# A layer norm that takes its mean from the first tiles: four norms of a two-block network on one core

## The chip, the cores and the metric

The kernel runs on one core of a Trainium2 chip. The metric is the device time of one launch in microseconds, the median of several runs. The kernel before took 2532.76 us (three runs, 2528.5 to 2535.85).

Engines are named as the profile names them: PE is TensorE's matmul (PEld its weight load), DVE is VectorE, ACT is ScalarE, SP is SyncE, whose queue starts the DMA transfers. An engine works its own list of instructions in order and waits at an instruction until what it needs is there.

## The reference

Two blocks follow one another; the change touches only the second. That is a trunk of two layers over 256 tokens of width 1024 and, beside them, 256 context tokens. A layer is

```python
def _layer_norm(x, g, b):
    mu = jnp.mean(xf, axis=-1, keepdims=True)
    var = jnp.mean(jnp.square(xf - mu), axis=-1, keepdims=True)
    return ((xf - mu) * lax.rsqrt(var + NORM_EPS) * g + b)
...
    y, yc = _token_mixer(x * (1 + scale1) + shift1, xc * (1 + cscale1) + cshift1, p, cos, sin, last)
    x = _layer_norm(DN_ALPHA * x + gate1 * y, p['ln1_g'], p['ln1_b'])
    x = _layer_norm(DN_ALPHA * x + gate2 * _conv_ffn(x * (1 + scale2) + shift2, p), p['ln2_g'], p['ln2_b'])
    if last:
        return x, None
    xc = _layer_norm(DN_ALPHA * xc + cgate1 * yc, p['ln1_g'], p['ln1_b'])
    xc = _layer_norm(DN_ALPHA * xc + cgate2 * _conv_ffn(xc * (1 + cscale2) + cshift2, p), p['ln2_g'], p['ln2_b'])
```

The token mixer is a gated linear attention, a latent attention and a convolution side by side, merged by an output projection; `_conv_ffn` is an up projection to twice 2816 columns, a short convolution, a gate and a down projection. The first layer needs both streams (0 is x, 1 is the context), the second only x.

## The kernel before

Features lie on the 128 partitions and tokens along the free dimension, so a stream is 8 tiles of 128 x 256 and a norm over features is a sum over partitions and tiles. Weights come from HBM in blocks (`wraw`, four buffers). ScalarE casts each block to a high part `wh` (line 284), VectorE subtracts to get the low part `wl` (line 285), three buffers each, so a cast waits until TensorE has released the block three before. Activations are split in the same way (`hx`: line 312 on ScalarE, line 313 on VectorE), and each product is three matmuls (lines 320, 321, 322).

`project` is the output projection of a layer and `down` the down projection of its feed-forward part, each one stream at a time. After each output tile an epilogue adds the residual (line 1225) and, from the second tile on, adds the tile into a running total (lines 1315 and 1383). When all eight tiles of a stream are there, `ln` runs: one matmul of the total with a matrix of -1/D gives minus the mean on all partitions (line 1170); each tile is shifted by it (VectorE, line 1172) and squared (ScalarE, line 1174, into one of four `lt` buffers); its column sums go to PSUM by small matmuls with a vector of ones (line 374, four records of the profile a tile). Then come the variance (line 384), a reciprocal root by integer start and two refinements on VectorE (lines 361 to 367), two transposes that spread the result over the partitions (line 379), and one product a tile (line 1180). `modulate` applies scale and shift (ScalarE, line 1145) and splits the result into `hx` for the next dense stage; the last norm instead goes to line 1889 (ScalarE) and from there to the output by DMA. In layer 1's start, line 1507 onwards make the gates of the linear attention.

`beside` is called within a norm and lets the next piece of work take a step: stream 1's projection beside stream 0's norm, stream 0's up projection beside stream 1's norm. In layer 1 there is one stream, so the norm after `project` has nothing beside it, and that after `down` is the end of the program. The order of instructions on each engine comes from a scheduler that works on the whole program; it isn't written out by hand.

Of the kernel before, what the change touches and what calls it, by code (L numbers as in the profile page):

```python
# [16 lines left out]
AF = mybir.ActivationFunctionType  # L17
ALU = mybir.AluOpType
# [3 lines left out]
P = 128  # L22
D = 1024
KT = 8
S = 256
# [3 lines left out]
EPS = 1e-6  # L29
# [166 lines left out]
class Body:  # L196
# [968 lines left out]
    def ln(self, pool, s, w, eps, total, beside):  # L1165
# [13 lines left out]
        for k in range(KT):  # L1179
            nc.vector.tensor_tensor(s[k], s[k], R, ALU.mult)  # L1180
            if k % 2:
                beside()

    def begin(self, l, hx):


        nc, tc = self.nc, self.tc
        key = f"v2{l}"
        n = 2 - l
        g = SimpleNamespace(hx=hx, hq=[(h[:, : S * n], w[:, : S * n]) for h, w in hx], od={}, ud={}, hb={}, ahead=True)  # L1190
        pool = lambda es, n, **k: es.enter_context(tc.tile_pool(name=f"{n}{l}", bufs=1, **k))
        g.mix, g.mix2, g.cin = [ExitStack() for _ in range(3)]
        g.lp = lp = pool(g.mix, "mix")
        self.mp = lambda: self.t(lp, [P, 2, 512], tag="M", bufs=4)

        for v in ("b_gates", "b_conv", "b_r", "conv_dw", "gla_norm_g"):
            a, k, L = self.vat[key][v]
            g.hb[v] = self.t(lp, [P, k * L], tag="h_" + v)
            nc.vector.tensor_scalar(g.hb[v], self.vt[key][:, a : a + k * L], 0.5, None, ALU.mult)
        x = self.v(key, "b_qk")[:, :, 0]  # L1200
        g.hb["b_qk"] = self.t(lp, x.shape, tag="n_b_qk")
        nc.vector.tensor_scalar(g.hb["b_qk"], x, 128.0 ** -0.5, None, ALU.mult)
        self.bp = pool(g.mix2, "mixb")
        self.ncv = 2 if l == 0 else 3
        g.Rc = self.psum(S * n, "sx")
        V = lambda v, k, i=0: self.vc(key, v, k, i)
        cin = pool(g.cin, "cin", side="right")
        g.decay, pre = self.gla_gates(l, cin, lp, hx, g.hb, V)
        g.work = self.conv_in(l, cin, g, V, list(range(n)), pre)
        return g  # L1210

    def layer(self, l, g, mod, xd, xo, nxt, late):


        nc, tc = self.nc, self.tc
        key = f"v2{l}"
        V = lambda n, k, i=0: self.vc(key, n, k, i)
        full = [0, 1] if l == 0 else [0]
# [58 lines left out]
        def beside(gp, i):  # L1277
            if l == 0:
                self.ada_all(1)
            taps(gp)  # L1280
# [22 lines left out]
        h2 = self.modulated()  # L1303
        s = [m2[:, i, :W] for m2 in [self.mp() for _ in range(4)] for i in range(2)]
        tiles = lambda st: [t[:, sl(st)] for t in s]
        sums = {}

        def project(st):
            x = tiles(st)
            sums[st] = total = self.t(lp, [P, S], tag="lt", bufs=4)  # L1310

            def epi_o(m, ps):
                residual(x[m], st, m, ps, xd, 16)
                if m:
                    nc.vector.tensor_tensor(total, x[0] if m == 1 else total, x[m], ALU.add)

            return self.dense_steps(f"w_o{l}", range(4), mx, epi_o, tok=lambda m: sl(st))

# [30 lines left out]
        for st in full:  # L1349
# [9 lines left out]
                    work = up(range(0, 6), sl(0))  # L1359
            beside = lambda: next(work, None)  # L1360
            x = tiles(st)
            self.ln(lp, x, S, EPS / 2, sums[st], beside)
            self.modulate(lp, x, sc, sh, st, h2, beside)
            for k in range(KT):
                nc.vector.tensor_scalar(x[k], x[k], V("ln1_g", k), V("ln1_b", k), ALU.mult, ALU.add)
# [9 lines left out]

        def down(st):
            x = tiles(st)
            sums[st] = total = self.t(lf, [P, S], tag="lt", bufs=4)

            def epi_d(m, ps):  # L1380
                residual(x[m], st, m, ps, xo, 40)
                if m:
                    nc.vector.tensor_tensor(total, x[0] if m == 1 else total, x[m], ALU.add)

            return self.dense_steps(f"w_dn{l}", range(KT), gx, epi_d, tok=lambda m: sl(st))

        work, out = down(0), None
        for st in full:
# [8 lines left out]
                    work = islice(out.work, 4)  # L1397
            beside = lambda: next(work, None)
            x = tiles(st)
            self.ln(lf, x, S, EPS / 2, sums[st], beside)  # L1400
            h = nxt(lf, x, st, beside)
            out = out or h
        return out, late2
# [601 lines left out]
```

## Time and profile before

| | before |
|---|---|
| median of 3 runs | 2532.76 us (2528.5 to 2535.85) |
| profiled execution | 2538.2 us, its span 2536.3 us |
| TensorE, VectorE, ScalarE busy | 97%, 72%, 50% of the span |
| mean granted TensorE clock | 0.984 |
| chain that ended last | TensorE 86%, VectorE 7%, DMA 3%, ScalarE 2% |
| largest groups of the chain | lines 320, 321, 322: 22%, 21%, 21%; line 374: 2% |

The table says where time could be won at all: TensorE is nearly always busy, so the share of the other engines counts only in the short stretches where TensorE waits for them. Four norms are touched by the change, and the prediction calls them by letters: A, layer 0, after `project` of stream 1 (about 1395 to 1450 us); B, layer 0, after `down` of stream 1 (about 1785 to 1870); C, layer 1, after `project` (about 2314 to 2340); D, layer 1, after `down`, the last of the program (from 2516). In a row of the timeline "x8" stands for eight instructions in a run, and what is in brackets is how long the engine stood idle before the row and which engine and line released it.

### The profile page before, as it was taken

What the parts mean: (1) busy time and instruction counts of PE and PEld (TensorE: products, weight loads), DVE (VectorE), ACT (ScalarE), POOL (GpSimd) and SP (SyncE); (2) the same over time, 40 slices, a digit from 0 to 9 for tenths busy, and PEclk for the clock granted to TensorE, in tenths of its full rate; (3) what the DMA queues carried; (4) which work ended last, traced back from release to release, by engine and by line L of the source; (5) the groups of instructions that cost most, each with busy time, mean ns of one, the idle gap of its engine ahead of it and who ended that gap; (6) DMA issues with size and microseconds to landing.
All of it is one profiled execution on the core that took longest, in us unless ns stands there. A gap on an engine that the chain in (4) does not pass through costs nothing.

```text
span 2536.3 us, 45917 instructions
## 1 busy us (share of the span) xinstructions
PE 2459.2 (97%) x18416; PEld 2108.9 (83%) x18416; DVE 1817.8 (72%) x3390; ACT 1260.5 (50%) x2252; POOL 0.2 (0%) x4
## 2 busy tenths in 40 slices
PE   7999999999999999999999999999989999998998
PEld 7577878998788888666889998899878897798997
DVE  8566568856777688786636876656786688777884
ACT  5432345655456532554433654444655645555653
POOL 0000000000000000000000000000000000000000
PEclk9999999999999999999999999999999999998998
DMA  6566466554321222432334542256342332365663
GB/s 205 193 232 233 141 200 202 189 182 142 108 88 59 67 94 80 163 121 79 125 108 158 171 150 92 98 187 192 132 145 74 105 129 70 125 197 167 193 198 110
DMA packets 125782, 361.53 MB, mean 143 GB/s; under 512 B 14209, under 2 KB 39681, under 8 KB 125441
## 3 DMA queue, kind: packets, MB, share of 16 engines
q1 hardware_dynamic: 125568, 358.60, 43.2%
q8 instruction: 145, 2.38, 0.4%
q14 instruction: 69, 0.56, 0.1%
HBM read 344.08 MB, written 14.46 MB: 141 GB/s over the span
## 4 chain that ended last, share of the span: by engine, by line
PE 86%; DVE 7%; DMA 3%; ACT 2%; issue 1%; SPq 0%; ACTq 0%; DVEq 0%
PE mm L320 22%; PE mm L322 21%; PE mm L321 21%; PE aux L374 2%; PE sy L1110 2%; DVE wl L285 2%; DVE cv L1461 2%; PE aux L1780 1%; PE aux L1661 1%; PE sy L1793 1%; PE aux L1779 1%; PE aux L1617 1%; PE mm L1582 1%; PE aux L748 1%; PE mm L1580 1%
## 5 line engine op out<-in xcount | busy, mean ns | idle before, releaser
L284 ACT CAST wh<-wraw 128x1024 fp32r<-128x1024 f32 (+3 forms) x544 | 543.5, 1000 | 739.2 <-PE mm L321 626.0
L285 DVE TENSOR_TENSOR wl<-wraw,wh 128x1024 fp32r<-128x1024 f32 (+3 forms) x544 | 631.9, 1163 | 327.2 <-ACT wh L284 313.9
L320 PE MATMUL mm<-hx,wh 128*128 128x256 f32 (+1 forms) x1816 | 607.3, 335 | 9.1 <-ACT wh L284 3.4
L322 PE MATMUL mm<-hx,wl 128*128 128x256 f32 (+1 forms) x1816 | 602.9, 333 | 5.6 <-DVE wl L285 5.4
L321 PE MATMUL mm<-hx,wh 128*128 128x256 f32 (+1 forms) x1816 | 603.5, 333 | 1.5 <-DVE hx L313 1.5
L320 PEld LDWEIGHTS mm<-hx,wh 128*128 128x128 f32 x1816 | 345.5, 191 | 47.0 <-issue 4.1
L322 PEld LDWEIGHTS mm<-hx,wl 128*128 128x128 f32 x1816 | 344.8, 190 | 43.1 <-DVE wl L285 7.0
L321 PEld LDWEIGHTS mm<-hx,wh 128*128 128x128 f32 x1816 | 345.3, 190 | 37.9 <-issue 4.0
L1461 DVE SCALAR_TENSOR_TENSOR cv<-u,h_conv_dw,cv 128x512 f32<-128x512 f32 (+1 forms) x480 | 295.4, 616 | 8.6
L320 PE MATMUL mm<-b,wh 128*128 128x256 f32 x688 | 200.1, 292 | 2.1 <-ACT b L312 1.8
L322 PE MATMUL mm<-b,wl 128*128 128x256 f32 x688 | 196.3, 286 | 1.4 <-DVE wl L285 1.4
L321 PE MATMUL mm<-b,wh 128*128 128x256 f32 x688 | 195.7, 285 | 0.6 <-DVE b L313 0.6
L320 PEld LDWEIGHTS mm<-b,wh 128*128 128x128 f32 x688 | 132.0, 193 | 19.2 <-issue 11.5
L321 PE MATMUL mm<-gx,wh 128*128 128x256 f32 x528 | 147.9, 280 | 0.0
L322 PE MATMUL mm<-gx,wl 128*128 128x256 f32 x528 | 147.8, 280 | 0.0
L320 PE MATMUL mm<-gx,wh 128*128 128x256 f32 x528 | 147.7, 280 | 0.0
L321 PE MATMUL mm<-sp,wh 128*128 128x256 f32 (+1 forms) x448 | 141.0, 315 | 0.1
L322 PE MATMUL mm<-sp,wl 128*128 128x256 f32 (+1 forms) x448 | 140.7, 314 | 0.1
L320 PE MATMUL mm<-sp,wh 128*128 128x256 f32 (+1 forms) x448 | 140.6, 314 | 0.0
L322 PEld LDWEIGHTS mm<-b,wl 128*128 128x128 f32 x688 | 131.9, 192 | 7.6 <-DVE wl L285 2.6
L321 PEld LDWEIGHTS mm<-b,wh 128*128 128x128 f32 x688 | 131.7, 192 | 4.4 <-DVE b L313 2.1
L322 PEld LDWEIGHTS mm<-gx,wl 128*128 128x128 f32 x528 | 99.4, 188 | 0.0
(546 smaller groups left out, 4476.6 us busy)
## 6 DMA issues: line engine op xcount, KB each, us to landing
wraw<-w_up SPq DMA_DIRECT2D x100, 512.0 KB, 3.5
wraw<-w_ada SPq DMA_DIRECT2D x88, 512.0 KB, 4.8
wraw<-w_gates SPq DMA_DIRECT2D x48, 512.0 KB, 3.5
wraw<-w_dn SPq DMA_DIRECT2D x48, 512.0 KB, 3.6
wraw<-f_up SPq DMA_DIRECT2D x44, 512.0 KB, 3.5
wraw<-w_in SPq DMA_DIRECT2D x34, 512.0 KB, 4.0
wraw<-w_conv SPq DMA_DIRECT2D x32, 512.0 KB, 3.6
wraw<-w_o SPq DMA_DIRECT2D x24, 512.0 KB, 3.5
```

The source lines that it names most:

```text
L284: nc.scalar.copy(h, raw)
L285: nc.vector.tensor_tensor(l, raw, h.bitcast(F32), ALU.subtract)
L320: mm(ps, wh, xh, start=first, stop=False)
L321: mm(ps, wh, xl, start=False, stop=False)
L322: mm(ps, wl, xh, start=False, stop=last)
L374: self.nc.tensor.matmul(pc[:, t : t + 1], sq[:, t * P : t * P + P], self.ones[:, 0:1], start=first and t == 0, stop=last and t == n - 1)
L748: mm(ps[q, i], lhs(8 * b + i, q), rhs(8 * b + i, q), start=True, stop=True)
L1110: nc.tensor.matmul(ps[q], self.sc[:, c : c + 32], w[:, i], start=j == 0 and k < nt, stop=j == len(lot) - 1 and k >= KT - nt)
L1461: nc.vector.scalar_tensor_tensor(r(o), u[:, :, j : j + S], dw(j), r(o), ALU.mult, ALU.add)
L1580: mm(ps, xh[:, tk], wh, start=kk == 0, stop=False)
L1582: mm(ps, xh[:, tk], wl, start=False, stop=kk == KT - 1)
L1617: mm(ps[r : r + b, s, j], ka[:, a : a + b], qa[:, c : c + b], start=True, stop=True)
```

## The change

For the last stream of each layer (`st == full[-1]`: stream 1 in layer 0, stream 0 in layer 1) the norms after `project` and after `down` are done by a new function `ln_ahead`. It takes as a provisional mean that of the first n tiles (n = 6 after `project`, 7 after `down`): the total of those tiles is scaled by 8/n on ScalarE and multiplied with the matrix of -1/D. All n tiles are shifted, squared and summed as soon as tile n-1 has its residual, and each later tile as soon as it has its own. The sums of the later tiles' shifted values are taken too (`pc[:, 2:4]`); from them follows how far the provisional mean is off. The variance is the mean square less the square of that offset, and the result is x times y plus b, where y is the reciprocal root and b is minus the offset times y. So a tile gets a product and an addition where it got a product.

```diff
+    def ln_ahead(self, x, total, n, pool):
...
+        def shifted(k):
+            nc.vector.tensor_tensor(x[k], x[k], st.R, ALU.add)
+            q = self.t(pool, [P, S], tag="lt", bufs=4)
+            nc.scalar.activation(q, x[k], AF.Square)
+            if k >= n:
+                self.colsum(st.pc[:, 2:4], x[k], False, False)
+            self.colsum(st.pc[:, 0:2], q, k == 0, k == KT - 1)
+
+        def taken(m):
+            if 0 < m < n:
+                nc.vector.tensor_tensor(total, x[0] if m == 1 else total, x[m], ALU.add)
+            if m == n - 1:
+                nc.scalar.activation(total, total, AF.Copy, scale=KT / n)
+                st.R, st.pc = self.psum(S, "aux"), self.psum(4, "aux")
+                nc.tensor.matmul(st.R, self.cc("negd", "c0"), total, start=True, stop=True)
+                for k in range(n):
+                    shifted(k)
+            elif m >= n:
+                shifted(m)
+
+        def done(eps, beside):
+            v, w, b = [self.t(self.sm, [P, 2], tag=t) for t in ("rsv2", "lnw", "lnb")]
+            nc.scalar.activation(w, st.pc[:, 2:4], AF.Square, scale=1.0 / D)
+            nc.vector.tensor_scalar(v, st.pc[:, 0:2], 1.0 / D, eps, ALU.mult, ALU.add)
+            nc.vector.tensor_tensor(v, v, w, ALU.subtract)
+            y = self.rsqrt(v, 2)
+            nc.vector.scalar_tensor_tensor(b, st.pc[:, 2:4], -1.0 / D, y, ALU.mult, ALU.mult)
+            beside()
+            R = self.psum(2 * S, "aux")
+            for i, c in enumerate((y, b)):
+                for t in range(2):
+                    self.rowcast(c, t, R[:, i * S + t * P : i * S + t * P + P])
+            beside()
+            for k in range(KT):
+                nc.vector.tensor_tensor(x[k], x[k], R[:, :S], ALU.mult)
+                nc.vector.tensor_tensor(x[k], x[k], R[:, S:], ALU.add)
+                if k % 2:
+                    beside()
...
         def project(st):
             x = tiles(st)
-            sums[st] = total = self.t(lp, [P, S], tag="lt", bufs=4)
+            taken = add_up(st, x, lp, 6)
...
-                if m:
-                    nc.vector.tensor_tensor(total, x[0] if m == 1 else total, x[m], ALU.add)
+                taken(m)
...
         def down(st):
             x = tiles(st)
-            sums[st] = total = self.t(lf, [P, S], tag="lt", bufs=4)
+            taken = add_up(st, x, lf, 7)
```

`add_up` returns `taken` of `ln_ahead` for the last stream and the old total otherwise; the old norm stays for stream 0 of layer 0. ScalarE's list has 24 table loads in the whole program where it had 22; the two new ones stand in the gate logs (line 1523 before).

The order moves with it. On ScalarE at A, the list before has stream 0's modulate (line 1145, with its cast, line 312) to the end, and then stream 1's eight squares, of which two stand here (line 1174; `M` are the tiles, `fsh` and `fsc` shift and scale, `wraw` and `wh` a weight block).

```order
L1145 ACTIVATE lt_14177<-M_13543,fsh_13535,fsc_13534 128x256
L1145 ACTIVATE lt_14181<-M_13544,fsh_13535,fsc_13534 128x256
L312 CAST hx_13539<-lt_14177 128x256
L312 CAST hx_13539<-lt_14181 128x256
L284 CAST wh_14344<-wraw_14342 128x1024
L1145 ACTIVATE lt_14185<-M_13544,fsh_13535,fsc_13534 128x256
L312 CAST hx_13539<-lt_14185 128x256
L284 CAST wh_14384<-wraw_14382 128x1024
L1174 ACTIVATE lt_14250<-M_13541 128x256
L1174 ACTIVATE lt_14255<-M_13541 128x256
```
In the changed kernel (line 1203 the scaling, line 1194 a square) the same place reads:

```order
L284 CAST wh_14313<-wraw_14311 128x1024
L284 CAST wh_14354<-wraw_14352 128x1024
L1203 ACTIVATE lt_13817<-lt_13817 128x256
L1194 ACTIVATE lt_14094<-M_13541 128x256
L1194 ACTIVATE lt_14099<-M_13541 128x256
L284 CAST wh_14396<-wraw_14394 128x1024
L1194 ACTIVATE lt_14104<-M_13542 128x256
L1194 ACTIVATE lt_14109<-M_13542 128x256
L1194 ACTIVATE lt_14114<-M_13543 128x256
L1194 ACTIVATE lt_14119<-M_13543 128x256
L1145 ACTIVATE lt_14123<-M_13541,fsh_13535,fsc_13534 128x256
L1145 ACTIVATE lt_14127<-M_13541,fsh_13535,fsc_13534 128x256
```
The squares of the first six tiles now stand ahead of the first modulate of stream 0, with one weight cast among them.

On TensorE at D, the list before ends the down projection (`gx` with `wh` and `wl`), and then has the mean and the column sums, of which two of the eight rows stand here.

```order
L321 MATMUL mm_26550<-gx_24739,wh_26613 128x256
L322 MATMUL mm_26550<-gx_24738,wl_26614 128x256
L320 MATMUL mm_26550<-gx_24740,wh_26613 128x256
L321 MATMUL mm_26550<-gx_24741,wh_26613 128x256
L322 MATMUL mm_26550<-gx_24740,wl_26614 128x256
L1170 MATMUL aux_26640<-lt_25934,v_c_2_75 128x256
L374 MATMUL aux_26641<-v_c_2_75,lt_26644 128x1 x2
L374 MATMUL aux_26641<-v_c_2_75,lt_26649 128x1 x2
```
In the changed kernel the first column sums stand within the last tile's matmuls (seven such rows in all, the mean matmul, line 1205, ahead of them):

```order
L320 MATMUL mm_26642<-gx_24229,wh_26645 128x256
L374 MATMUL aux_26605<-v_c_2_75,lt_26608 128x1 x2
L321 MATMUL mm_26642<-gx_24230,wh_26645 128x256
L322 MATMUL mm_26642<-gx_24229,wl_26646 128x256
L320 MATMUL mm_26642<-gx_24231,wh_26675 128x256
L374 MATMUL aux_26605<-v_c_2_75,lt_26613 128x1 x2
```
and after its last matmul only the last tile's two sums, of the shifted tile (`ring`) and of its square (`lt`), and four transposes are left:

```order
L320 MATMUL mm_26642<-gx_24793,wh_26705 128x256
L321 MATMUL mm_26642<-gx_24794,wh_26705 128x256
L322 MATMUL mm_26642<-gx_24793,wl_26706 128x256
L374 MATMUL aux_26605<-v_c_2_75,ring_25986 128x1 x2
L374 MATMUL aux_26605<-v_c_2_75,lt_26730 128x1 x2
L379 MATMUL aux_26757<-v_c_2_75,rsy_4329_26744 128x128 x2
L379 MATMUL aux_26757<-v_c_2_75,lnb_26740 128x128 x2
```
Eight column sums and the mean came after the last matmul; now two sums do, and the transposes are four, two of the root and two of `lnb`.

## Rows read from the trace of the kernel before

**Rows 1.** The page: span, TensorE's busy time, the chain that ended last by engine.
```profile
span 2536.3 us, 45917 instructions
...
PE 2459.2 (97%) x18416; PEld 2108.9 (83%) x18416; DVE 1817.8 (72%) x3390; ACT 1260.5 (50%) x2252; POOL 0.2 (0%) x4
...
PE 86%; DVE 7%; DMA 3%; ACT 2%; issue 1%; SPq 0%; ACTq 0%; DVEq 0%
```

**Rows 2.** Timeline at D: start us, us, engine line op out<-in, idle before <-releaser.
```profile
2516.44 0.28 PE L322 MATMUL mm<-gx,wl 128*128 128x256 f32 x1
...
2516.76 0.48 DVE L1225 SCALAR_TENSOR_TENSOR ring<-mm,mod,ring 128x256 f32<-128x256 f32 x1 [5.87 <-PE mm L322]
...
2518.50 2.74 DVE L1172 TENSOR_TENSOR ring<-ring,aux 128x256 f32<-128x256 f32 x8 [0.79 <-PE aux L1170]
...
2519.42 6.50 PE L374 MATMUL aux<-v_c,lt 128*128 128x1 f32 x32 [0.96 <-ACT lt L1174]
...
2525.95 0.16 DVE L384 TENSOR_SCALAR rsv<-aux 128x2 f32<-128x2 f32 x1 [4.71 <-PE aux L374]
...
2528.23 0.66 PE L379 MATMUL aux<-v_c,rsy 128*128 128x128 f32 x2 [2.32 <-DVE rsy L367]
...
2529.00 2.74 DVE L1180 TENSOR_TENSOR ring<-ring,aux 128x256 f32<-128x256 f32 x8 [0.91 <-PE aux L379]
...
2529.46 4.04 ACT L1889 ACTIVATE ring<-ring,v_v 128x256 f32<-128x256 f32 x8 [6.45 <-DVE ring L1180]
```

**Rows 3.** Timeline at C.
```profile
2314.14 0.28 PE L322 MATMUL mm<-sp,wl 128*128 128x256 f32 x1
...
2323.50 0.16 DVE L384 TENSOR_SCALAR rsv<-aux 128x2 f32<-128x2 f32 x1 [4.21 <-PE aux L374]
...
2328.06 0.69 ACT L312 CAST hx<-lt 128x256 fp32r<-128x256 f32 x2
...
2328.50 1.01 PE L320 MATMUL mm<-hx,wh 128*128 128x256 f32 x3 [2.06 <-ACT hx L312]
```

**Rows 4.** Windows at A (two) and B: busy us (instructions) of each engine, PEclk, DMA.
```profile
1405.00:1415.00 10.00, 8.08 (x49) 7.47 (x48) 7.31 (x20) 4.26 (x10) 0.00 (x0) 0.78 0.51 175
1447.00:1449.00 2.00, 0.40 (x4) 0.19 (x2) 2.00 (x6) 1.71 (x3) 0.00 (x0) 1.00 0.62 193
1836.00:1838.00 2.00, 0.00 (x0) 0.00 (x0) 2.00 (x5) 2.00 (x4) 0.00 (x0) 0.83 0.00 0
```

**Rows 5.** Chain of waits within 1370 to 1440 (stream 0's norm among matmuls).
```profile
1379.15 0.57 PE aux L1170 x2
...
1384.57 0.34 PE aux L374 x4
```

**Rows 6.** Window at C.
```profile
2320.00:2332.00 12.00, 7.46 (x33) 6.71 (x33) 7.12 (x27) 5.35 (x14) 0.00 (x0) 0.50 0.00 1
```

**Rows 7.** Timeline at A.
```profile
1394.83 1.09 ACT L1145 ACTIVATE lt<-M,fsh,fsc 128x256 f32<-128x256 f32 x2 [0.18 <-DVE M L1180]
...
1400.33 0.48 DVE L1225 SCALAR_TENSOR_TENSOR M<-mm,mod,M 128x256 f32<-128x256 f32 x1
...
1405.80 0.28 PE L320 MATMUL mm<-hx,wh 128*128 128x256 f32 x1
...
1405.88 1.05 ACT L284 CAST wh<-wraw 128x1024 fp32r<-128x1024 f32 x1 [0.62 <-PE mm L321]
...
1409.36 5.83 PE L374 MATMUL aux<-v_c,lt 128*128 128x1 f32 x32 [1.37 <-ACT lt L1174]
```

**Rows 8.** Timeline at B.
```profile
1797.87 0.50 PE L374 MATMUL aux<-v_c,lt 128*128 128x1 f32 x4
...
1817.06 0.43 DVE L313 TENSOR_TENSOR hx<-lt,hx 128x256 fp32r<-128x256 f32 x1
...
1822.36 1.28 ACT L1523 ACT_TABLE_LOAD   x1
...
1823.66 1.06 ACT L1523 ACTIVATE sp<-sp 128x1024 f32<-128x1024 f32 x1
```

More of the change, by code (lines that the diff above doesn't have):

```diff
@@ L1182, in ln @@
                 beside()
+    def ln_ahead(self, x, total, n, pool):
+        nc = self.nc
+        st = SimpleNamespace()
+        def shifted(k):
[34 more added lines that the diff above has]
+                    beside()
+        return taken, done
     def begin(self, l, hx):
@@ L1305, in layer, with add_up, taken, norm @@
         tiles = lambda st: [t[:, sl(st)] for t in s]
-        sums = {}
+        sums, ahead = {}, []
+        def add_up(st, x, pool, n):
+            sums[st] = total = self.t(pool, [P, S], tag="lt", bufs=4)
+            if st == full[-1]:
+                taken, done = self.ln_ahead(x, total, n, pool)
+                ahead.append(done)
+                return taken
+            def taken(m):
+                if m:
+                    nc.vector.tensor_tensor(total, x[0] if m == 1 else total, x[m], ALU.add)
+            return taken
+        def norm(pool, x, st, beside):
+            if st == full[-1]:
+                ahead.pop()(EPS / 2, beside)
+            else:
+                self.ln(pool, x, S, EPS / 2, sums[st], beside)
         def project(st):
             x = tiles(st)
-            sums[st] = total = self.t(lp, [P, S], tag="lt", bufs=4)
+            taken = add_up(st, x, lp, 6)
             def epi_o(m, ps):
                 residual(x[m], st, m, ps, xd, 16)
-                if m:
-                    nc.vector.tensor_tensor(total, x[0] if m == 1 else total, x[m], ALU.add)
+                taken(m)
             return self.dense_steps(f"w_o{l}", range(4), mx, epi_o, tok=lambda m: sl(st))
@@ L1361, in layer @@
             x = tiles(st)
-            self.ln(lp, x, S, EPS / 2, sums[st], beside)
+            norm(lp, x, st, beside)
             self.modulate(lp, x, sc, sh, st, h2, beside)
@@ L1377, in down @@
             x = tiles(st)
-            sums[st] = total = self.t(lf, [P, S], tag="lt", bufs=4)
+            taken = add_up(st, x, lf, 7)
             def epi_d(m, ps):
                 residual(x[m], st, m, ps, xo, 40)
-                if m:
-                    nc.vector.tensor_tensor(total, x[0] if m == 1 else total, x[m], ALU.add)
+                taken(m)
             return self.dense_steps(f"w_dn{l}", range(KT), gx, epi_d, tok=lambda m: sl(st))
@@ L1399, in layer @@
             x = tiles(st)
-            self.ln(lf, x, S, EPS / 2, sums[st], beside)
+            norm(lf, x, st, beside)
             h = nxt(lf, x, st, beside)
```

## The prediction

> **What bounds the kernel now.** I read the page first. TensorE is busy for 2459.2 of the 2536.3 us of the span, and in the chain that ended last it holds 86% and VectorE 7% [rows 1]. So a change that takes work off other engines pays only where TensorE stands still, and every instruction that is added to TensorE costs its duration. Next I read the timelines around the four norms that are changed. I call them A (layer 0, after the output projection, stream 1), B (layer 0, after the down projection, stream 1), C (layer 1, after the output projection) and D (the last norm of the program). They differ in what lies beside them.
>
> D stands alone. The last down matmul ends at 2516.44 + 0.28 = 2516.72, and the program ends 19.6 us later [rows 1, 2]. In between the reader sees a serial chain: residual, total, mean, eight shifts, column sums for 6.50 us, 2.28 us of small VectorE operations for the reciprocal root (2525.95 to 2528.23), eight products, output. C is alone as well, but only until the first up matmul: the last projection matmul ends at 2314.42, the small operations start at 2323.50 (9.08 later), and the first matmul on hx starts at 2328.50 [rows 3]. At A and B stream 1's norm lies beside stream 0's work, so there the question is which engine's queue is full. At A, 40 us later, TensorE is busy for 0.40 of 2 us while VectorE is busy for all of it, and at B a stretch of 2 us has no matmul at all and VectorE full [rows 4]. These two places pay for VectorE work.
>
> **D, step by step.** Added to TensorE ahead of the last matmul: one mean matmul and seven tiles' column sums. Where stream 0's norm is already interleaved with matmuls, the pair of records of a mean matmul costs 0.57 in the chain and a tile's column sums 0.34 [rows 5]. So 0.57 + 7 x 0.34 = 2.95 us, and the last matmul ends that much later. The seven shifts and squares themselves lie beside the last tile's matmuls, during which VectorE is free (its residual waits 5.87 us for TensorE [rows 2]).
> After it: residual 0.52 (with its start), shift 0.42, then the square; from the first shift to the first column sum before it is 0.92 (2518.50 to 2519.42), so the last square's sum starts 0.54 + 0.92 = 1.46 after the last matmul, and with about 0.5 for itself the small operations start at about 2.1. They are 13 where 11 were: the one before the first row cast adds 2.28 / 11 = 0.2, so the cast starts at 2.1 + 2.5 = 4.6. A cast takes 0.77 until its reader starts (2528.23 to 2529.00); the second one follows. The first product starts at 5.4, the first addition perhaps 0.3 later than it could. Then 16 VectorE operations at 2.74 / 8 = 0.34 end at about 11.3, where 8 took 2.74. ScalarE's last output operation takes another 0.6, and from its end to the end of the span stay 2.8 us (2529.46 + 4.04 = 2533.50 to 2536.3). Together 14.7 after the last matmul instead of 19.6: -4.9 + 2.95 = **-1.9 us**. If nothing came early, the eight additions would cost 2.74 more on VectorE, of which some 1.2 hides because ScalarE's outputs were pacing (4.04 against 2.74 [rows 2]), plus 0.2, plus 0.3: +2.0 at worst. At best the column sums slip into gaps that the weight loads leave and D gives -2.5.
>
> **C.** Six tiles' sums stand ahead of the last matmul: 0.57 + 6 x 0.34 = 2.6 later. The last two tiles bring four sums behind it. By the same steps as at D the small operations start about 2.5 after the last matmul, so 5.2 where 9.08 was: -3.9, plus 0.2 for one more operation. The eight additions (2.74) lie on VectorE between the cast and the up matmuls; there VectorE was busy 7.12 of 12 us, at a TensorE clock of 0.50 [rows 6], so the 4.9 idle us take them. If that cover were gone they would cost 1.9, because VectorE would pace hx. Something returns later, where the next weight block waits for VectorE; I take 0.7. **-3.0**, between -3.7 (nothing returns) and -1.1 (that cover gone).
>
> **A.** Off TensorE goes the run of column sums at a lower clock (5.83 us for 32 records [rows 7]); on it come ten tiles' sums (eight of squares, two of shifted tiles) at 0.34, 3.4: -2.4. VectorE gets eight additions and loses two totals: 6 x 0.34 = +2.0, and it is the engine that TensorE waits for in this stage [rows 4], so I count 2.0 in full. The third term is order. Before, stream 0's modulate starts at 1394.83, ahead of tile 5's residual at 1400.33, and the first hx matmul comes at 1405.80 [rows 7]. Now six squares stand ahead of that modulate on ScalarE. They can't start before tile 5's residual (1400.81), total, scaling and mean matmul, about 1402.4; with six squares at 0.42 and a weight cast of 1.05 between them the modulate starts near 1406.3, and the first hx is ready near 1407.3. TensorE wants it at 1405.80 + 2.6 = 1408.4. So 10 us of slack shrink to one, while two more squares and weight casts (each about 0.4 and 1.05 [rows 7]) stand between the following modulates. A wait there is between 0 and 4; I take 2. **+1.6**, from -4.3 (no wait, VectorE's work hidden, and the 1.9 idle us of 1405 to 1415 [rows 4] close as well) to +3.6.
>
> **B.** Here VectorE is full. Eight additions less one total: 7 x 0.34 = +2.4 on the engine that TensorE waits for [rows 4]. Column sums were already interleaved, at 0.50 a tile [rows 8]; nine sets at 0.34 now stand for eight at 0.50: -0.9. ScalarE's list has two more table loads in the gate logs. Such a load takes 1.28 us on the engine, and the activation next to it starts 0.02 us after its end (1822.36 + 1.28, then 1823.66 [rows 8]). Two are 2.6 us beside VectorE's work; I let half of it through, 1.3.
> The Trainium skill (ScalarE: Activation LUTs, What ACT_TABLE_LOAD costs) adds a drain of about 1380 ns to each load. By that rule the estimate is 5.3 us for two, and B would lose 1.3 us more; the trace shows no such gap between load and activation, and my sum goes by the row.
> Seven squares also stand ahead of six of stream 0's eight modulates. I take that as hidden, since VectorE is what is late here. B is 2.4 - 0.9 + 1.3 = **+2.8**. It is -0.9 if VectorE's work and the loads hide. At the other end the six modulates with their casts come behind the last square: a pair of modulates takes 1.09 and a pair of casts 0.69 on ScalarE [rows 3, 7], so 6 x 0.89 = 5.3 us, by which hx of stream 1 (complete at 1817.49 [rows 8]) and the gate chain behind it are later still; with both loads in full that is 2.4 - 0.9 + 2.6 + 5.3 = +9.4.
>
> **Sum.** -1.9 - 3.0 + 1.6 + 2.8 = -0.5 us. The profiled execution took 2538.2, which is its span of 2536.3 and 1.9 around it; the median of the three runs is 2532.76, 5.4 lower, and they lie 7.4 apart. So 2537.7 for an execution like the profiled one, and 2532 for a median.
>
> **Rivals.**
> 1. *The overlaps close the waits at A and B* (faster). The squares' early start lets stream 1's hx follow at once, and no modulate is late. For it: TensorE idles 1.9 us in ten at A. Against it: VectorE's full stretches. A -4.3, B -0.9, C -3.7, D -2.5: -11.4, so 2521.
> 2. *The modulate behind the squares decides* (slower). ScalarE works its list in order, and six or seven squares wait there for the mean while stream 0's hx, which TensorE needs next, stands behind them. For it: the order of the changed kernel shows just that. Against it: 10 us of slack at A. It decides once hx of stream 0 comes more than a microsecond later than worked out above. A +3.6, B +9.4, C and D -4.9: +8.1, so 2540.9, just past the bound.
> 3. *The squares don't come early* (the change does not do what it says). The scaling of the total stands behind weight casts on ScalarE, which wait for TensorE to release a weight buffer; then the mean arrives when the last tile is done. For it: at A two casts stand directly ahead of the scaling in ScalarE's list. Against it: the scaling has one or two tiles of matmuls to get through, and at D VectorE alone waits 5.87 us for the last one [rows 2]. Added VectorE work stays: A +2.0, B +2.4, C +0.5, D +2.0, about +6.9, so 2539.7.
>
> **Chances and range.** About 0.3%, 7.6 us, is what a measurement of this kernel can tell from no change: 2525.2 to 2540.4. My forecast, in which the gains of layer 1 and the losses of layer 0 cancel, gets 0.62; rival 1 gets 0.16, rival 2 0.12, and rival 3 0.10, of which most lies inside the bound. Faster 0.16, same 0.71, slower 0.13 (rival 2, and a little of rival 3). The range runs from 2524 to 2541, which leaves out most of rival 1 and the tail of rival 2.
>
> **What would show it.** At D: 9 pairs of sums where 8 stood, seven of them before the last L322, the small operations starting about 2 us after that matmul, 16 products and additions in 5.5 us, and the end about 14.7 us behind the last matmul. At C: first hx matmul about 8.2 us after the last projection matmul instead of 14.1 (which itself ends 2.6 later). At A: when stream 0's modulate starts (1406 forecast), whether TensorE waits for hx there, and how long VectorE stays full until 1450. At B: the end of stream 1's hx, and how long VectorE stays full behind it. The prediction is wrong if A and B together lose more than 12 us or gain more than 3, or if at D the sums come after the last matmul.

## The result: slower, and the loss sits at three of the four places

The changed kernel takes 2552.38 us (median of 6 runs, 2546.43 to 2555.31), the kernel before 2534.31 in the same comparisons (2527.72 to 2539.51). The ratio is 1.0058, 95% interval 1.0037 to 1.0080. The forecast was 2532 and no change, with a range from 2524 to 2541.

The page of the changed kernel's profiled execution answers to [rows 1]:

```profile
span 2550.5 us, 46024 instructions
...
PE 2458.2 (96%) x18448; PEld 2101.7 (82%) x18448; DVE 1829.3 (72%) x3424; ACT 1270.8 (50%) x2262; POOL 0.2 (0%) x4
...
PE 85%; DVE 7%; ACT 3%; DMA 2%; issue 1%; SPq 0%; ACTq 0%; DVEq 0%
```

So the change costs 0.58%, clear of the noise. The span is 14.2 us longer, but TensorE is busy a microsecond less: it stands still for 92.3 us where it was 77.1. To see where, I number the weight matmuls (lines 320 to 322, 11904 in each trace) and take how much later the n-th starts than in the trace of before. What this lag grows by over a place is the place's loss: A from the 5400th to the 5790th, B from the 7836th to the 8400th, C from the 10284th to the 10428th, D from the 11832nd to the end. All figures in the table are us against the first trace of before, one execution each.

| kernel | A | B | C | D | ratio of times to before (95%) |
|---|---|---|---|---|---|
| forecast of the change | +1.6 | +2.8 | -3.0 | -1.9 | |
| changed | +6.5 | +7.2 | +2.5 | +0.2 | 1.0058 (1.0037 to 1.0080) |
| e1 layer 1 only | -0.3 | +0.8 | +3.1 | +0.2 | 1.0013 (0.9994 to 1.0031) |
| e2 layer 0 late | +4.8 | +7.5 | +2.7 | +0.2 | 1.0038 (1.0021 to 1.0055) |
| e3 no additions | +2.4 | +6.7 | -1.7 | -2.3 | 1.0019 (0.9997 to 1.0041) |
| e4 paired | +6.6 | +6.4 | +1.0 | -0.6 | 1.0041 (1.0016 to 1.0067) |
| e5 late, no additions | +2.2 | +0.3 | 0.0 | -2.2 | 0.9981 (0.9960 to 1.0003) |
| e6 third tile after | 0.0 | +1.1 | +0.4 | +0.2 | one run, 2535.46 us |
| e7 squares summed on VectorE | -0.1 | -0.5 | -0.3 | -3.4 | one run, 2532.39 us |
| e8 raw squares | +1.7 | +1.6 | -4.0 | -4.0 | 1.0019 (0.9999 to 1.0039) |
| e9 = e8 again | +0.1 | +1.5 | -3.3 | -4.4 | 1.0031 (1.0008 to 1.0054) |
| e10 = before again | -1.7 | +0.6 | 0.0 | -1.3 | one run, 2530.53 us |
| e11 e8 with seven memsets | +1.7 | +1.3 | -3.3 | -4.4 | 1.0008 (0.9992 to 1.0024) |
| e12 = e7 again | -0.2 | +2.6 | +0.3 | -3.4 | 1.0005 (0.9986 to 1.0024) |

Places where a kernel has the old norm (A and B in e1 and e6 to e12) scatter from -1.7 to +2.6. Smaller differences at A and B aren't read from this table. At C and D kernels with the same norm in layer 1 agree within 0.7, apart from C in e3 and e5 (-1.7 and 0.0) and from D of before, which e10 repeats at -1.3. The changed kernel's four places add up to 16.4 us, and its execution was 14.2 longer: the places hold the loss. The stretches between them came out at +3.7, +1.8, -3.4 and -4.4, so that the two figures lie so close is partly luck; in e10, the same program as before, the stretch between B and C alone is -5.9.

The scatter is mostly TensorE's clock, which is granted at one of two levels, 2.4 or 1.2 GHz. The same places by the time that TensorE stands idle and the time that its clock spends at 1.2 GHz (us; "old norm" are the other executions with the old norm in that place, e1 and e6 to e12 at A and B, e10 at C):

| | before | old norm | changed | e2 late | e3 no additions | e4 paired | e5 both |
|---|---|---|---|---|---|---|---|
| A, TensorE idle | 4.8 | 4.7 to 5.1 | 9.4 | 7.1 | 7.0 | 9.4 | 4.2 |
| A, at 1.2 GHz | 10.2 | 6.8 to 13.7 | 13.7 | 13.7 | 10.2 | 17.1 | 13.7 |
| B, TensorE idle | 11.5 | 10.0 to 11.8 | 17.2 | 17.4 | 13.3 | 13.0 | 10.8 |
| B, at 1.2 GHz | 17.1 | 17.1 to 23.9 | 20.5 | 20.5 | 27.3 | 23.9 | 17.1 |
| C, TensorE idle | 6.9 | 6.9 | 8.8 | 8.8 | 5.9 | 8.5 | 5.9 |
| C, at 1.2 GHz | 13.7 | 13.7 | 13.7 | 13.7 | 10.2 | 13.7 | 13.7 |

At A the old norm lost -1.7 with 6.8 us at 1.2 GHz, -0.3 to +0.1 with 10.2, and +1.7 with 13.7. Its idle time there moves by 0.4. So at A idle time tells causes apart that the losses can't.

**D.** Columns as in [rows 2].

```profile
2534.47 0.28 PE L322 MATMUL mm<-gx,wl 128*128 128x256 f32 x1
...
2534.78 0.48 DVE L1273 SCALAR_TENSOR_TENSOR ring<-mm,mod,ring 128x256 f32<-128x256 f32 x1 [7.09 <-PE mm L322]
...
2537.15 0.16 DVE L1214 TENSOR_SCALAR rsv<-aux 128x2 f32<-128x2 f32 x1 [1.43 <-ACT lnw L1213]
...
2539.63 0.66 PE L379 MATMUL aux<-v_c,rsy 128*128 128x128 f32 x2 [2.72 <-DVE rsy L367]
...
2540.75 0.42 DVE L1225 TENSOR_TENSOR ring<-ring,aux 128x256 f32<-128x256 f32 x1 [1.07 <-PE aux L379]
...
2541.21 0.42 DVE L1226 TENSOR_TENSOR ring<-ring,aux 128x256 f32<-128x256 f32 x1
...
2541.55 0.41 DVE L1225 TENSOR_TENSOR ring<-ring,aux 128x256 f32<-128x256 f32 x1
...
2546.72 0.42 DVE L1226 TENSOR_TENSOR ring<-ring,aux 128x256 f32<-128x256 f32 x1
...
2547.18 0.60 ACT L1955 ACTIVATE ring<-ring,v_v 128x256 f32<-128x256 f32 x1 [0.19 <-DVE ring L1226]
```

From the end of the last matmul (2534.75) to the end of the span are 15.7 us, where 14.7 was forecast and 19.6 stood before. The variance starts after 2.4 us (2.1 forecast), and the first product after 6.0 (5.4 forecast). The sixteen operations then take 6.4 us, not 5.5: an addition starts 0.44 to 0.46 after the product that it reads, the next product 0.34 after the addition. Ahead of the last matmul the reader sees what a set of column sums costs:

```profile
2527.00 0.27 PE L320 MATMUL mm<-gx,wh 128*128 128x256 f32 x1
2527.11 0.50 PE L374 MATMUL aux<-v_c,lt 128*128 128x1 f32 x4
2527.47 0.36 PE L321 MATMUL mm<-gx,wh 128*128 128x256 f32 x1
2527.67 0.28 PE L322 MATMUL mm<-gx,wl 128*128 128x256 f32 x1
2527.79 0.28 PE L320 MATMUL mm<-gx,wh 128*128 128x256 f32 x1
```

From L320 to the next L320 are 0.79, and without the sums three matmuls take 0.35: 0.44 a tile, where [rows 5] had given 0.34. Seven sets and the mean matmul make the last matmul 4.0 us later, not 2.95. So D is -3.8 + 4.0.

The -3.8 is flattered by the trace that it's measured against. There the clock fell to 1.2 GHz 3.3 us after the last matmul, early in the old norm's column sums, which took 6.50 us [rows 2]. In e10, the same program, it fell after 4.7 us, and the sums took 5.21:

```profile
2513.03 5.21 PE L374 MATMUL aux<-v_c,lt 128*128 128x1 f32 x32 [0.96 <-ACT lt L1174]
```

Against e10 every D of the table is 1.3 worse.

**C.**

```profile
2333.52 0.28 PE L322 MATMUL mm<-sp,wl 128*128 128x256 f32 x1
...
2337.72 0.16 DVE L1214 TENSOR_SCALAR rsv<-aux 128x2 f32<-128x2 f32 x1 [1.70 <-ACT lnw L1213]
...
2343.38 1.01 PE L320 MATMUL mm<-hx,wh 128*128 128x256 f32 x3 [2.10 <-ACT hx L312]
...
2354.28 0.28 PE L322 MATMUL mm<-hx,wl 128*128 128x256 f32 x1
...
2357.53 0.36 PE L320 MATMUL mm<-hx,wh 128*128 128x256 f32 x1 [2.98 <-DVE ring L1404]
```

The first hx matmul comes 9.6 us after the last projection matmul (14.1 in [rows 3]), and with 3.5 us of sums ahead of it 1.0 us earlier than before. That gain is gone 11 us later. The clock is at 1.2 GHz for the first 5.9 us of the hx matmuls (3.8 before), and 0.7 of the gain goes there. (e10 shows the same without any change: its first hx matmul came 1.3 earlier, the clock was low for 6.5 us, and C was 0.0.) Then TensorE waits 2.98 us, for which before has no counterpart.

**A.** First the variance of the kernel before, then the changed kernel:

```profile
1415.22 0.16 DVE L384 TENSOR_SCALAR rsv<-aux 128x2 f32<-128x2 f32 x1 [2.92 <-PE aux L374]
```

```profile
1420.24 0.77 PE L374 MATMUL aux<-v_c,lt 128*128 128x1 f32 x4
...
1421.05 0.60 ACT L1145 ACTIVATE lt<-M,fsh,fsc 128x256 f32<-128x256 f32 x1 [2.39 <-PE aux L374]
...
1422.69 0.15 DVE L1214 TENSOR_SCALAR rsv<-aux 128x2 f32<-128x2 f32 x1
...
1439.29 0.35 PE L320 MATMUL mm<-hx,wh 128*128 128x256 f32 x1 [3.13 <-DVE ring L1404]
```

The squares came early, yet the variance (line 1214) comes late: it was worked out 23.1 us after the 5400th weight matmul before and 26.9 us after it now. The last tile's sum (1420.24) stands in TensorE's list behind 19 up matmuls, and ScalarE waits 2.39 for it, because squares and modulates share the four `lt` buffers. Later TensorE waits 3.13 for line 1404, the line of the wait at C.

**B.** First the kernel before, then the changed one:

```profile
1792.78 0.48 DVE L1225 SCALAR_TENSOR_TENSOR ring<-mm,mod,ring 128x256 f32<-128x256 f32 x1
...
1802.75 0.16 DVE L384 TENSOR_SCALAR rsv<-aux 128x2 f32<-128x2 f32 x1 [3.65 <-PE aux L374]
...
1806.31 0.40 PE L379 MATMUL aux<-v_c,rsy 128*128 128x128 f32 x2
...
1807.56 1.74 DVE L1180 TENSOR_TENSOR ring<-ring,aux 128x256 f32<-128x256 f32 x5
```

```profile
1809.26 0.48 DVE L1273 SCALAR_TENSOR_TENSOR ring<-mm,mod,ring 128x256 f32<-128x256 f32 x1
...
1814.57 0.15 DVE L1215 TENSOR_TENSOR rsv<-rsv,lnw 128x2 f32<-128x2 f32 x1
...
1820.78 0.41 PE L379 MATMUL aux<-v_c,rsy 128*128 128x128 f32 x2
...
1821.43 0.42 DVE L1225 TENSOR_TENSOR ring<-ring,aux 128x256 f32<-128x256 f32 x1 [0.61 <-PE aux L379]
...
1822.30 0.40 DVE L1226 TENSOR_TENSOR ring<-ring,aux 128x256 f32<-128x256 f32 x1
...
1822.62 0.41 DVE L1225 TENSOR_TENSOR ring<-ring,aux 128x256 f32<-128x256 f32 x1
...
1824.08 0.41 DVE L1226 TENSOR_TENSOR ring<-ring,aux 128x256 f32<-128x256 f32 x1
...
1837.73 0.41 DVE L313 TENSOR_TENSOR hx<-lt,hx 128x256 fp32r<-128x256 f32 x1
...
1882.03 0.58 PE L322 MATMUL mm<-hx,wl 128*128 128x256 f32 x1 [5.84 <-DVE wl L285]
```

From the last residual to the variance were 10.0 us, now 5.3. But the residual itself comes 4.5 later against the same matmul, since the squares' sums stand among the down matmuls. So the variance is no earlier (18.6 and 18.4 us after the 7836th weight matmul). Then the small operations take longer (3.6 us to the row cast before, 6.2 now), other work standing between them. The products, of which the first five came 0.33 apart, are 1.0 to 1.8 apart, with additions and other work between; hx of stream 1 is complete at 42.0, not 33.3 [rows 8]. The longest wait comes 44 us behind that: TensorE stands 5.84 us for a low part of a weight (line 285), which VectorE makes only after a run of the gates' and the convolution's operations. The longest wait for line 285 in the place was 1.4 before.

### The profile page after: what moved, and what is told of

Read it like the earlier page. It is cut to its first block, busy times and chain, and to the rows that moved or that the text cites. A ratio compares the mean times of both kernels' runs of the same rounds, so it can differ in the third digit from the quotient of the medians.

```text
span 2550.5 us, 46024 instructions
## 1 busy us (share of the span) xinstructions
PE 2458.2 (96%) x18448; PEld 2101.7 (82%) x18448; DVE 1829.3 (72%) x3424; ACT 1270.8 (50%) x2262; POOL 0.2 (0%) x4
## 4 chain that ended last, share of the span: by engine, by line
PE 85%; DVE 7%; ACT 3%; DMA 2%; issue 1%; SPq 0%; ACTq 0%; DVEq 0%
PE mm L320 21%; PE mm L321 21%; PE mm L322 21%; PE aux L374 2%; PE sy L1110 2%; DVE wl L285 2%; DVE cv L1527 2%; PE aux L1846 2%; PE aux L1727 1%; PE sy L1859 1%; PE aux L1845 1%; PE aux L1683 1%; PE mm L1648 1%; PE mm L1646 1%; PE mm L1647 1%
## 5 line engine op out<-in xcount | busy, mean ns | idle before, releaser
L320 PE MATMUL mm<-hx,wh 128*128 128x256 f32 (+1 forms) x1816 | 607.3, 336 | 18.0 <-DVE ring L1404 6.1
L320 PEld LDWEIGHTS mm<-hx,wh 128*128 128x128 f32 x1816 | 347.6, 192 | 59.8 <-issue 7.4
L320 PE MATMUL mm<-b,wh 128*128 128x256 f32 x688 | 198.3, 290 | 2.8 <-ACT b L312 1.8
L320 PE MATMUL mm<-gx,wh 128*128 128x256 f32 x528 | 147.5, 279 | 0.0
L320 PEld LDWEIGHTS mm<-b,wh 128*128 128x128 f32 x688 | 131.4, 192 | 18.4 <-issue 10.8
L320 PE MATMUL mm<-sp,wh 128*128 128x256 f32 (+1 forms) x448 | 140.5, 314 | 0.0
L321 PEld LDWEIGHTS mm<-gx,wh 128*128 128x128 f32 x528 | 99.3, 188 | 0.1
```

The lines of the kernel that those rows point to most:

```text
L320: mm(ps, wh, xh, start=first, stop=False)
L321: mm(ps, wh, xl, start=False, stop=False)
```

## The experiments

Theory "order": at A and B the squares ahead of stream 0's modulate, on ScalarE, cost. Rival "work": the additions on VectorE do. For C: "the three up tiles end together", against "VectorE's backlog".

**e1, layer 1 only.** In both places `if st == full[-1]` becomes

```diff
-            if st == full[-1]:
+            if l == 1:
```

> The new norm only in layer 1 (C and D); layer 0 keeps the old norm. By the traces of before and after, TensorE loses 6.4 us at A and 7.2 at B, 2.7 at C and 0.2 at D. If the four places add up, A and B are as before and this kernel is 2.9 us over before (ratio 1.001). Rival: the loss isn't in the places but in the whole run's pace, then it stays near 1.006.

Measured: A and B are as before, C +3.1, D +0.2, ratio 1.0013 (0.9994 to 1.0031). The places add up; layer 0 holds most of the loss.

**e2, layer 0 late.**

```diff
         def taken(m):
...
+            if late:
+                return
+            start(m)
+
+        def start(m):
             if m == n - 1:
...
         def done(eps, beside):
+            if late:
+                for m in range(n - 1, KT):
+                    start(m)
```

> In layer 0 all shifts, squares and sums are issued when the norm is taken up, not with the tile's epilogue: the same instructions as in the changed kernel, on ScalarE behind stream 0's modulate as before. Layer 1 as in the changed kernel. If the order on ScalarE is what costs (squares ahead of the modulate), A falls from +6.4 to at most +2.5 and B from +7.2 to at most +3, the whole to about 2540. If VectorE's added work costs, A stays at +5 or more, B at +6, and the whole at 2549.

Measured: A +4.8, B +7.5. The order alone doesn't explain B. At A its 1.7 is within the scatter, but TensorE's idle time falls from 9.4 to 7.1, half of what the change had added (4.8 before).

**e3, no additions.**

```diff
-                nc.vector.tensor_tensor(x[k], x[k], R[:, S:], ALU.add)
```

> Leaves out the eight additions of the offset after the product at all four places (so the result lacks the correction of the mean). If VectorE's added work is what costs at A and B, each falls by 2.5 or more; if the order on ScalarE does, A stays above +4.5. At C hx is then as fast as before: if the interleaving of the first three up tiles costs there, the list of TensorE goes back to ending them one after another and C goes from +2.7 to about -2; if it is only VectorE's backlog, C goes to about 0. At D the tail is 2.5 to 3.7 shorter than in the changed kernel's 15.7.

Measured: A falls by 4.1 to +2.4. Of this 2.3 is idle time of TensorE; the rest goes with 10.2 instead of 13.7 us at 1.2 GHz, a difference that the old norm's executions show too. So at A work and order cost about the same. B stays at +6.7: the work alone doesn't explain B either. C is -1.7, and the order of lines 320 to 322 in TensorE's list is the old one again, as the first theory for C has it. (e5, with the same norm in layer 1, has 0.0 at C; its idle time there is the same 5.9, against 8.8 in the changed kernel, and the rest is clock.) D is -2.3, its tail 13.2.

**e4, paired.**

```diff
-            for k in range(KT):
-                nc.vector.tensor_tensor(x[k], x[k], R[:, :S], ALU.mult)
-                nc.vector.tensor_tensor(x[k], x[k], R[:, S:], ALU.add)
-                if k % 2:
-                    beside()
+            for k in range(0, KT, 2):
+                for j in (k, k + 1):
+                    nc.vector.tensor_tensor(x[j], x[j], R[:, :S], ALU.mult)
+                for j in (k, k + 1):
+                    nc.vector.tensor_tensor(x[j], x[j], R[:, S:], ALU.add)
+                beside()
```

> Two products, then two additions, instead of product and addition by turns: the same instructions, but no addition stands directly behind the product that it reads. At D the 16 operations take 5.5 us instead of 6.4, so the tail is 14.8 instead of 15.7. At C TensorE's list now takes the first three up tiles one after another. If the three tiles ending together cost there, the wait of 3 us for the fourth tile goes and C falls from +2.7 to about -1.5; if VectorE's backlog does, it stays near +2. At A and B little is expected, between -1 and +1 against the changed kernel.

Measured, at D on VectorE (1226 the product, 1228 the addition):

```profile
2530.67 0.75 DVE L1226 TENSOR_TENSOR ring<-ring,aux 128x256 f32<-128x256 f32 x2 [1.07 <-PE aux L379]
...
2531.34 0.75 DVE L1228 TENSOR_TENSOR ring<-ring,aux 128x256 f32<-128x256 f32 x2
...
2535.31 0.75 DVE L1228 TENSOR_TENSOR ring<-ring,aux 128x256 f32<-128x256 f32 x2
```

From 2530.67 to the end at 2536.06 are 5.4 us: four operations take 1.33 instead of 1.58. D is -0.6. At C the wait ahead of the fourth tile is gone, but with one tile after another TensorE now waits 2.2 us for the low part of hx in the first: C is +1.0, where -1.5 was expected.

**e5, late and no additions** (e2 and e3 together).

> Layer 0 late as in e2, and the eight additions of the offset left out at all four places as in e3 (so the result lacks the correction of the mean). At B neither step alone helped: the lag grew by 7.5 us with the late order and by 6.7 without the additions, against 7.2. If each of the two holds hx of stream 1 back far enough by itself, B falls to at most 2 with both gone, and A to at most 1. If something else of the new norm costs at B (its two more small operations, the second pair of row casts, the scaling), B stays at 5 or more.

Measured: B +0.3, A +2.2. At A TensorE's idle time is back at 4.2, and what is left is about as much as the old norm loses with 13.7 us at 1.2 GHz (+1.7). For B the events, in us after the 7836th weight matmul:

| | before | changed | e2 late | e3 no additions | e5 both |
|---|---|---|---|---|---|
| last residual | 8.6 | 13.1 | 8.6 | 13.1 | 8.6 |
| variance | 18.6 | 18.4 | 18.4 | 18.4 | 18.4 |
| row cast | 22.1 | 24.6 | 22.6 | 24.6 | 22.6 |
| hx of stream 1 complete | 33.3 | 42.0 | 39.6 | 35.5 | 34.0 |
| loss at B | | +7.2 | +7.5 | +6.7 | +0.3 |

So at B two causes stand in each other's shadow: with either of them gone the loss stays near 7 us, with both gone it is 0.3. Additions alone (e2) make hx 6.3 later, and TensorE's idle time grows by 5.9 us. Early squares alone (e3) make hx 2.2 later, and idle time grows by only 1.8; the rest of e3's 6.7 is clock, 27.3 us at 1.2 GHz where before has 17.1. The first spell, of 6.8 us, begins in the wait for hx (2.67 us). A late hx alone isn't enough for that: in e10 it is complete at 34.8, 1.5 late, and B is +0.6. No execution with the old norm has more than 23.9 us at 1.2 GHz here. But e3 has one trace, and that its clock falls so each time isn't shown.

**e6, third up tile after the second** (on e1).

```diff
-                    for k, ((wh, wl), (xh, xl)) in enumerate(zip(w, x)):
+                    with self.after(mybir.EngineType.PE) if m == third else nullcontext():
+                        for k, ((wh, wl), (xh, xl)) in enumerate(zip(w, x)):
...
```

> The new norm only in layer 1, and at C the third up tile's matmuls are held behind the second's, so the three no longer end together; the instructions are those of e1. If the three tiles ending together is what costs at C, the wait of 3.0 us before the fourth tile goes and C falls from +3.1 (e1) to between -0.5 and +0.5. If VectorE's additions cost by themselves, the wait only moves to hx and C stays near +3. D as in e1, +0.2.

Measured: C +0.4 where e1 has +3.1, with the same instructions. First e1, then e6:

```profile
2348.87 0.36 PE L320 MATMUL mm<-hx,wh 128*128 128x256 f32 x1 [2.96 <-DVE ring L1404]
```

```profile
2339.69 0.28 PE L322 MATMUL mm<-hx,wl 128*128 128x256 f32 x1
2340.58 0.36 PE L320 MATMUL mm<-hx,wh 128*128 128x256 f32 x1 [0.61 <-DVE ring L1406]
```

The wait ahead of the fourth tile is 0.61, not 2.96. So the order of three tiles was the loss of C: taken k by k they end together, and the fourth waits until VectorE's epilogue has read the results of one of them (line 1404 here and in the changed kernel, 1406 in e6).

**e7 and e12, squares summed on VectorE** (on e6 and e4).

```diff
             if k >= n:
                 self.colsum(st.pc[:, 2:4], x[k], False, False)
-            self.colsum(st.pc[:, 0:2], q, k == 0, k == KT - 1)
+                self.colsum(st.pc[:, 0:2], q, False, k == KT - 1)
+            elif k == 0:
+                st.q = q
+            else:
+                nc.vector.tensor_tensor(st.q, st.q, q, ALU.add)
+                if k == n - 1:
+                    self.colsum(st.pc[:, 0:2], st.q, True, False)
```

> The new norm only in layer 1; the squares of the first n tiles are added up on VectorE beside the last tiles' matmuls, and one column sum goes to TensorE instead of six or seven; products and additions paired as in e4, third up tile as in e6. If the column sums among the last matmuls are what takes the gain of D back (4.0 us later there), the last matmul is only about 1.1 us later and D falls from +0.2 to about -3.7; C falls by 2.5 to about -1.5. If VectorE can't hide six additions beside the last tile, D stays above -2.

> The kernel of e7, timed: its one execution took 2532.4, and its places C and D gave -0.3 and -3.4 us at the pace of 113.3 ns a matmul in the last up stage, where the kernel before has 117.8 (4.4 us less there). If places and pace add up and belong to the build, it is 5 to 8 us under before (ratio 0.997 to 0.998). If what was seen in one execution was chance, it is within 2 us of before.

Measured: D -3.4 both times, the last matmul 1.3 later instead of 4.0; the sums among the matmuls were what took D's gain. C gains less than expected (-0.3, +0.3): TensorE's waits there are 10.0 us where e6 has 6.4. Timed, the kernel is as fast as before: 1.0005 (0.9986 to 1.0024).

**e8, e9 and e11, raw squares.** In layer 1 a tile's square needs no mean:

```diff
+        def taken(m):
...
+            nc.scalar.activation(q, x[m], AF.Square)
+            if m == 0:
+                st.q = q
+            else:
+                nc.vector.tensor_tensor(st.q, st.q, q, ALU.add)
+            if m == KT - 1:
+                st.R, st.pc = self.psum(S, "aux"), self.psum(4, "aux")
+                nc.tensor.matmul(st.R, self.cc("negd", "c0"), total, start=True, stop=True)
+                self.colsum(st.pc[:, 2:4], total, True, False)
+                self.colsum(st.pc[:, 0:2], st.q, False, True)
```

The shifts then go beside the root, and one product a tile follows. e9 is the same kernel again; in e11 `nc.vector.memset(self.sc, 0.0)` at the start stands eight times.

> Layer 1 only, and the squares are of the unshifted tiles, so they need no mean: ScalarE squares a tile as it comes, VectorE adds the squares up, and the variance is the mean square less the squared mean (exact mean, no offset). After the root there is one product a tile again, and the shifts lie beside the root's small operations. Nothing is put among the last matmuls. If the additions behind the root and the sums among the matmuls are what ate the gain of the early squares, D falls to about -5 (tail 14 to 14.5 us), C to about -5, and the whole is 10 us under before (ratio 0.996). If the gain is eaten by something else, C and D stay above -2.

> The kernel of e8 once more, unchanged. C and D gave back 4.0 us each there, but matmuls took longer where nothing is changed: a median of 118.7 ns a matmul of 256 columns in the up stages against 113.3 in most of the other kernels and 117.8 before, at a granted clock of 1.00. If the pace comes anew with each execution, this profile shows another pace and the median moves towards 2527; if it belongs to the build, the pace is 118.7 again and the median stays near 2544.

> The kernel of e8 with seven more small memsets at its start on VectorE (below 1 us in all), which shift the program and nothing else. If the pace hangs on the build, it may come out as 113.3 or 117.8 here, and with it the whole falls by 5 to 10 us to about 2530 to 2535; C and D keep their -4.0. If the pace comes with the execution, the median is that of e8 and e9.

Measured at D (1199 the mean, 1206 the variance, 1211 a shift, 1217 a product):

```profile
2528.09 0.28 PE L322 MATMUL mm<-gx,wl 128*128 128x256 f32 x1
...
2529.40 0.70 PE L1199 MATMUL aux<-lt,v_c 128*128 128x256 f32 x2 [1.04 <-DVE lt L1190]
...
2531.13 0.16 DVE L1206 TENSOR_SCALAR rsv<-aux 128x2 f32<-128x2 f32 x1 [0.57 <-ACT lnw L1205]
...
2531.20 0.41 DVE L1211 TENSOR_TENSOR ring<-ring,aux 128x256 f32<-128x256 f32 x1
...
2535.73 2.74 DVE L1217 TENSOR_TENSOR ring<-ring,aux 128x256 f32<-128x256 f32 x8 [0.84 <-PE aux L379]
```

The last matmul isn't delayed, the variance comes 2.8 us after it, shifts lie between the small operations, and one run of products follows. C gives -4.0, -3.3 and -3.3, D -4.0, -4.4 and -4.4, somewhat under the 5 expected. Yet the kernel isn't faster: 1.0019, 1.0031 (1.0008 to 1.0054) and 1.0008. Some 8 us gained at C and D are lost where nothing was changed. Most of that is the pace of matmuls at full clock, as the section on the hardware shows; why the pace differs is open.

**e10, before again.**

> The kernel before, profiled once more. By the theory that the pace belongs to the build, the up stages show 117.8 ns again and matmuls of 512 columns 228.9; by the theory that it comes with the execution, some stages show 113.3.

Measured: 117.8 and 228.9 again, and the differences from before in the table.

## Why the prediction was wrong

It summed durations in isolation and booked what it didn't add as hidden. By its own sign, more than 12 us lost at A and B together, it is wrong with 13.7. Step by step:

- **D, the sums ahead of the last matmul**: 2.95 forecast, 4.0 measured. The 0.34 of [rows 5] is a share of the chain; the cost to TensorE's list is 0.44, as the rows of the changed kernel show. Summing on VectorE takes 2.7 of the 4.0 away (e7).
- **D, sixteen operations at 0.34**: 5.5 forecast, 6.4 measured. The row of eight independent operations in [rows 2] doesn't price a product with its addition directly behind; in pairs they do take 5.4 (e4). Another 0.6 was lost ahead of the first product.
- **C, "Something returns later ... I take 0.7"**: the step that failed most. From the first hx matmul to the end of the place 3.5 came back: some 0.7 by the clock and 3.0 in the fourth tile's wait. The forecast took the first up tiles' order as given; with hx coming at one tile a microsecond, the order became three tiles k by k, and without that C is 2.7 lower (e1 against e6). The sums cost 3.5 instead of 2.6, and the first hx matmul comes 9.6 after the last projection matmul instead of 8.2 (the steps of the prediction's sum give 7.7). Together the forecast of -3.0 became +2.5.
- **A, the gain of 2.4**: it didn't come. With as much time at 1.2 GHz as before, TensorE was busy for 57.5 us of the place in e3 and for 57.3 before, so the new sums cost it what the old ones had; and the variance is later than before, behind up matmuls and shared buffers. The two terms that were booked as losses are about right in idle time: the additions 2.3 (e3) for 2.0, the order 2.3 (e2) for 2, though stream 0's modulate starts 14.1 us later against the 5400th weight matmul than before, and 11.5 was forecast. The rest of +6.5 is busy time at the lower clock, within the scatter of the old norm.
- **B, "I take that as hidden"**: failed. With the modulate late, additions spread out and hx 8.7 us late, the place went to +7.2, inside the stated end of +9.4 but not at the 2.8. Idle time grew by 5.7 in the changed kernel and by 5.9 in e2, but by 1.8 and 1.5 in e3 and e4, where the time at 1.2 GHz grew by 10.2 and 6.8 instead. So the loss comes as waits or as clock, and only without both causes (e5) are both back. The loss doesn't need the two extra table loads: e2, e3 and e4 have 22 loads as before and lose 6.4 to 7.5 at B. So the 1.3 for them has no run that shows it; what they add in the changed kernel wasn't tried by itself. The longer figure of the Trainium skill (ScalarE: Activation LUTs, What ACT_TABLE_LOAD costs) would only have raised that term, and no run here shows its drain.

The second rival came nearest, with chance 0.12 and 2540.9: late modulates at layer 0. But it needed C and D to give 4.9 back, and its mechanism is at most half of what happened. The third rival, that the squares don't come early, holds at A and B in a form that I hadn't written: they came early and the variance did not.

The range missed because the four places weren't independent in their errors. Each was priced as if the rest of its engine's list stood still, and each was too low, by 2.1 to 5.5 us.

## What to carry to other kernels

Before work is moved ahead, follow the last input of the result that is to come early. Here it was the last tile's sum, and it came no earlier where TensorE had other work, however early seven of eight were done. Price what is put among the bottleneck's instructions by the pitch of that engine's own list with and without it, and look at the new list where several tiles share buffers: if they end together, the next one waits. Compare idle time and time at the lower clock separately; here the first repeated from one execution of a program to the next, and the second scattered. An operation added behind the critical result costs in full; one moved in front of it, as the raw squares' shifts, costs little.

## What the runs showed of the hardware

With a granted clock of 1.00 and TensorE full, matmuls of 256 columns came at different paces. The last up stage in 40 us of before, of the changed kernel and of e8 (busy us and number of matmuls of PE first, then the other engines, PEclk behind them):

```profile
2350.00:2390.00 40.00, 40.00 (x342) 40.00 (x341) 35.31 (x59) 25.58 (x42) 0.00 (x0) 1.00 0.62 188
```

```profile
2370.00:2410.00 40.00, 40.00 (x356) 40.00 (x355) 36.66 (x60) 27.00 (x45) 0.00 (x0) 1.00 0.66 197
```

```profile
2365.00:2405.00 40.00, 40.00 (x339) 40.00 (x339) 34.87 (x57) 25.63 (x43) 0.00 (x0) 1.00 0.60 185
```

That are 342, 356 and 339 matmuls, on average 117.8, 113.3 and 118.7 ns from one start to the next. Before showed 117.8 in both its traces, the three traces of raw squares 118.7, in every up stage; the kernels nearer to the change show 113.3 in some stages and 117.8 in others. e7 and e12 are the same program and differ: in the last up stage 113.3 and 117.8. So neither "it belongs to the build" nor "it comes with the execution" fits all of it, and the memsets of e11 changed nothing. Matmuls of 512 columns in layer 0's up stage came every 228.9 ns in both traces of before, every 232.4 to 233.3 in the others. 4.4 ns over the thousand matmuls of the last up stage are 4.4 us, as much as a place here. In the trace of the changed kernel the last up stage gained that much, which hid part of its loss.

The pace accounts for most of what the raw squares lost elsewhere. I compared the distance from each weight matmul to the next with before, wherever neither trace has a wait or the lower clock between the two (at most 130 ns for 256 columns, 250 for 512), and added the differences up outside the four places. They are +9.2, +8.3 and +9.8 us in e8, e9 and e11, -0.2 in e10 and -7.8 in the changed kernel. By the ratios less the four places, e8, e9 and e11 lost 9.5, 13.9 and 6.7 us there, each give or take 5. The timed executions point the same way: time multiplied by the mean granted clock is 2503 us for the raw squares in all three runs, and 2491 to 2494 for the kernel before beside the experiments. Nothing here shows what sets the pace.
